# GELU into the output tile, whole-tile instructions and a pinned ACT order in a split GELU-multiply kernel

## Chip, cores and metric

The kernel runs on one core of one Trainium2 chip. The metric is device time in microseconds (us) of one execution. The profile is of one such execution; its span is some 2 us shorter than that execution's time (470.1 against 471.85 before).

## The reference

```python
x = np.random.randn(32, 512, 2048)           # float32
x1, x2 = x[..., :1024], x[..., 1024:]
out = 0.5 * x1 * (1 + erf(x1 / np.sqrt(2))) * x2    # GELU(x1) * x2, float32
```

There are 134.2 MB to read and 67.1 MB to write, and one GELU and one multiply for each output element.

## The kernel before

The rows are cut into 16 tiles of 128 partitions x 8 rows. A partition's 8 rows are adjacent in memory. There are two input tiles and two output tiles. Loads are issued from SP (SyncE), stores from ACT (ScalarE; the last two tiles' from SP), GELU runs on ACT and the multiply on DVE (VectorE).

```python
R = 8
xpool = ctx.enter_context(tc.tile_pool(name="xpool", bufs=2))
opool = ctx.enter_context(tc.tile_pool(name="opool", bufs=2))
# ... load(i): sync.dma_start of a whole tile; store(queue, i, o_tile, rows)
ahead = [load(0), load(1)]
for i in range(n_tiles):
    x_tile = ahead.pop(0)
    o_tile = opool.tile([P, R, half], out.dtype, name="o_tile")
    last = i == n_tiles - 1
    for lo, hi in ((0, 1), (1, 2), (2, 4), (4, 8)) if last else ((0, 4), (4, 8)):
        rows = slice(lo, hi)
        nc.scalar.activation(out=x_tile[:, rows, :half], in_=x_tile[:, rows, :half], func=GELU)
        nc.vector.tensor_mul(out=o_tile[:, rows, :], in0=x_tile[:, rows, :half], in1=x_tile[:, rows, half:])
        if last and hi % 4 == 0:
            store(nc.sync, i, o_tile, slice(hi - 4, hi))
    if not last:
        store(nc.sync if i == n_tiles - 2 else nc.scalar, i, o_tile, slice(0, R))
    if i + 2 < n_tiles:
        ahead.append(load(i + 2))
```

Two rules of reuse follow from this. The load of tile i+2 can be issued only when the multiply of tile i has read its input tile. An output tile can be overwritten only when the store two tiles back has landed.

## Time and profile before

| | before |
|---|---|
| time, median of 3 (lowest to highest) | 471.61 us (471.43 to 471.72) |
| span of the profile | 470.1 us |
| busy: DVE, ACT | 30%, 25% |
| DMA queues' packets, both queues | 99.4% of 16 engines' span |

A queue of transfers must be read with two numbers: how long a transfer takes from issue to landing, and how much of that it spends behind others. The first is in the page's last part; here are the two rows for the bulk of the transfers (the last number is the median in us from issue to landing):

```profile
out_dram<-o_tile ACTq DMA_DIRECT2D x14, 4096.0 KB, 41.6
...
x_tile<-in_x_dram SPq DMA_DIRECT2D x16, 45.4
```

A load takes 45.4 us and a store 41.6, while a load and a store together land every 29 us. So on average 1.6 loads and 1.4 stores are under way: in the steady stretch there is always one of each, and part of the time a second stands behind it.

### The profile page before, as it was taken

What the parts mean: (1) busy time and instruction counts of PE and PEld (TensorE: products, weight loads), DVE (VectorE), ACT (ScalarE), POOL (GpSimd) and SP (SyncE); (2) the same over time, 40 slices, a digit from 0 to 9 for tenths busy, and PEclk for the clock granted to TensorE, in tenths of its full rate; (3) what the DMA queues carried; (4) which work ended last, traced back from release to release, by engine and by line L of the source; (5) the groups of instructions that cost most, each with busy time, mean ns of one, the idle gap of its engine ahead of it and who ended that gap; (6) DMA issues with size and microseconds to landing.
All of it is one profiled execution on the core that took longest, in us unless ns stands there. A gap on an engine that the chain in (4) does not pass through costs nothing.

```text
span 470.1 us, 217 instructions
## 1 busy us (share of the span) xinstructions
DVE 140.5 (30%) x34; ACT 115.4 (25%) x35; POOL 0.2 (0%) x4
## 2 busy tenths in 40 slices
DVE  0070703307043070420705106061150601507042
ACT  1051406024060230603206032060410605105060
POOL 0000000000000000000000000000000000000000
DMA  8999999999999999999999999999999999999988
GB/s 357 446 446 357 443 449 446 402 443 449 402 446 441 435 457 404 432 418 485 407 424 421 488 407 413 432 488 407 402 443 482 413 402 443 472 424 402 480 380 346
DMA packets 4754, 201.35 MB, mean 428 GB/s; under 512 B 528, under 2 KB 528, under 8 KB 528
## 3 DMA queue, kind: packets, MB, share of 16 engines
q1 hardware_dynamic: 2736, 142.61, 70.5%
q10 hardware_dynamic: 2016, 58.72, 28.9%
q14 instruction: 2, 0.02, 0.0%
HBM read 134.22 MB, written 67.11 MB: 428 GB/s over the span
## 4 chain that ended last, share of the span: by engine, by line
DMA 77%; DVE 14%; ACT 7%; issue 0%; ACTq 0%; SPq 0%
DMA x_tile<-in_x_dram 77%; DVE o_tile L58 14%; ACT x_tile L55 7%; ACTq L94 0%; SPq L42 0%; ACTq L55 0%
## 5 line engine op out<-in xcount | busy, mean ns | idle before, releaser
L58 DVE TENSOR_TENSOR o_tile<-x_tile 128x4096 f32<-128x4096 f32 (+2 forms) x34 | 140.5, 4171 | 321.2 <-ACT x_tile L55 321.2
L55 ACT ACTIVATE x_tile<-x_tile 128x4096 f32<-128x4096 f32 (+2 forms) x34 | 114.2, 3407 | 341.0 <-DMA x_tile<-in_x_dram 341.0
L55 ACT ACT_TABLE_LOAD x1 | 1.3, 1283 | 0.7 <-PEq L83 0.7
L83 POOL MEMSET const-bfloat16-1.0<- 128x1 bf16 x1 | 0.1, 102 | 0.0
L83 POOL MEMSET const-uint8-127<- 128x1 uint8 x1 | 0.1, 102 | 0.0
L83 POOL MEMSET const-float32-0.0<- 128x1 f32 x1 | 0.1, 99 | 0.2 <-issue 0.2
L83 POOL MEMSET const-float32-1.0<- 128x1 f32 x1 | 0.1, 99 | 0.0
## 6 DMA issues: line engine op xcount, KB each, us to landing
out_dram<-o_tile ACTq DMA_DIRECT2D x14, 4096.0 KB, 41.6
out_dram<-o_tile SPq DMA_DIRECT2D x1, 4096.0 KB, 24.8
out_dram<-o_tile SPq DMA_DIRECT2D x2, 2048.0 KB, 8.0
x_tile<-in_x_dram SPq DMA_DIRECT2D x16, 45.4
```

The source lines that it names most:

```text
L55: nc.scalar.activation(out=x_tile[:, rows, :half], in_=x_tile[:, rows, :half], func=GELU)
L58: nc.vector.tensor_mul(out=o_tile[:, rows, :], in0=x_tile[:, rows, :half], in1=x_tile[:, rows, half:],)
L83: nc = _bacc.Bacc("TRN2", target_bir_lowering=False, num_devices=1)
```

## The change

The change writes GELU to the output tile and multiplies there in place, handles tiles 1 to 14 with one GELU and one multiply each, joins the first two small steps of the last tile, and asks the scheduler to keep GELU at its place in program order, behind the store before it. The intent is fewer instructions and no second write into the input tile.

```diff
-        for lo, hi in ((0, 1), (1, 2), (2, 4), (4, 8)) if last else ((0, 4), (4, 8)):
+        if last:
+            steps = (0, 2), (2, 4), (4, 8)
+        else:
+            steps = ((0, 4), (4, 8)) if i == 0 else ((0, 8),)
+        for lo, hi in steps:
             rows = slice(lo, hi)
-            nc.scalar.activation(
-                out=x_tile[:, rows, :half], in_=x_tile[:, rows, :half], func=GELU
+            tc.keep_in_program_order(
+                nc.scalar.activation(
+                    out=o_tile[:, rows, :], in_=x_tile[:, rows, :half], func=GELU
+                )
             )
             nc.vector.tensor_mul(
                 out=o_tile[:, rows, :],
-                in0=x_tile[:, rows, :half],
+                in0=o_tile[:, rows, :],
                 in1=x_tile[:, rows, half:],
             )
```

## The prediction

> **What bounds the kernel now.** I read the page first: it says which resource has no free time.
>
> ```profile
> span 470.1 us, 217 instructions
> DVE 140.5 (30%) x34; ACT 115.4 (25%) x35; POOL 0.2 (0%) x4
> ...
> DMA  8999999999999999999999999999999999999988
> ...
> q1 hardware_dynamic: 2736, 142.61, 70.5%
> q10 hardware_dynamic: 2016, 58.72, 28.9%
> ...
> HBM read 134.22 MB, written 67.11 MB: 428 GB/s over the span
> ```
>
> The two compute engines are busy 30% and 25% of the span; the DMA row is 9 (90% or more) in all but three slices. The two queues' packets take 70.5% + 28.9% = 99.4% of the time of the 16 DMA engines: 0.6% of 470.1 us, some 3 us, is all the idle time there is. q1 holds the loads (and the last tiles' stores), q10 the other stores. The bytes are what the reference needs (134.2 MB in, 67.1 MB out, each once).
>
> The chain of waits must be read beside that. It lists compute in every second tile:
>
> ```profile
> 161.26 3.62 ACT x_tile L55
> 164.88 0.02 issue
> 164.91 8.77 DVE o_tile L58 x2
> 173.68 0.02 issue
> 173.70 45.52 DMA x_tile<-in_x_dram
> 219.22 0.02 issue
> 219.24 0.02 ACTq L55
> 219.25 0.04 issue
> 219.30 3.62 ACT x_tile L55
> ```
>
> A load takes 45.52 us from issue to landing, but 8.39 MB (134.22 MB over 16 loads) at 433 GB/s would need 19.4 us. So the link is mostly queueing. The chain is a closed loop with stretchable DMA pieces, not a row of fixed costs. The test is the rate over whole periods. A tile comes every 29.04 us (tile i+2's GELU starts 58.04 us after tile i's: 161.26, 219.30). Cut into such periods, the table by stretches says:
>
> ```profile
> 58.00:87.04 29.04, 8.76 (x2) 7.12 (x2) 0.00 (x0) 1.00 1.00 433
> ...
> 203.20:232.24 29.04, 8.76 (x2) 7.12 (x2) 0.00 (x0) 1.00 1.01 436
> ...
> 377.44:406.48 29.04, 8.76 (x2) 7.12 (x2) 0.00 (x0) 1.00 1.00 432
> ```
>
> The last two columns are DMA share and GB/s: share 1.00, 432 to 436 GB/s, while DVE works 8.76 and ACT 7.12 of 29.04 us. The kernel is bound by the rate of the DMA engines from the first load to the last store.
>
> **What the Trainium skill says.** "DMA: Bandwidth & Descriptors", section "Where 436 GB/s comes from", puts the ceiling of a core's 16 ports at 435.2 GB/s; the periods above are at it. The same page, "Queues, rings and completion order", says each DMA engine round-robins between its queues by packet. The trace agrees: load and store progress together, one 8.39 MB load and one 4.19 MB store landing per period, and neither queue starves. "VectorE: DVE Perf Modes", section on the TRN2 errata, gives (N+151)/0.96 ns for an fp32 two-tensor operation: 4424 ns at N = 4096, where the trace has 4422. "ScalarE: Activation LUTs", section "What ACT_TABLE_LOAD costs", gives 186 + 0.833 N ns without pointer operands: 3598 ns at 4096, where the trace has a mean of 3608.
>
> **The change part by part.** The durations come from the groups by shape:
>
> ```profile
> L58 DVE TENSOR_TENSOR o_tile<-x_tile 128x4096 f32<-128x4096 f32 x31 | 135.8, 4422 | 304.6 <-ACT x_tile L55 304.6
> L55 ACT ACTIVATE x_tile<-x_tile 128x4096 f32<-128x4096 f32 x31 | 110.4, 3608 | 320.6 <-DMA x_tile<-in_x_dram 320.6
> ...
> L58 DVE TENSOR_TENSOR o_tile<-x_tile 128x2048 f32<-128x2048 f32 x1 | 2.3, 2293 | 0.4 <-ACT x_tile L55 0.4
> ...
> L55 ACT ACTIVATE x_tile<-x_tile 128x2048 f32<-128x2048 f32 x1 | 1.9, 1895 | 0.0
> ```
>
> *Whole-tile instructions, tiles 1 to 14.* Two instructions of 4096 elements become one of 8192 on each engine. Extrapolated from these rows: ACT 3608 + 4096 x (3608 - 1895)/2048 = 7034 ns (the page's formula: 7010); DVE 4422 + 4096 x (4422 - 2293)/2048 = 8680 ns (8691). Busy time hardly changes: ACT 7.12 to 7.02, DVE 8.76 to 8.69. What changes is overlap: the multiply now waits for the whole GELU. From landing to freed tile it was 12.50 us (219.24 to 231.74, where the load and store are issued); it becomes 0.06 + 7.02 + 0.02 + 8.69 + 0.02 = 15.81, so **3.3 us longer per tile**, in 14 tiles.
>
> Does that reach the DMA? A load issued at 231.74 stands behind its predecessor, which lands at 248.3 (the next GELU starts at 248.35): 16.6 us of slack. The store issued at 231.74 stands behind the store issued at 202.80, which lands 41.7 us later, at 244.5: 12.8 us of slack. Both exceed 3.3; they shrink to about 13.3 and 9.5 us, and the DMA engines see no gap. The loads' time to landing should fall from 45.4 to about 42.1 us, the stores' from 41.6 to about 38.3, with landings at the same moments. Cost: 0.
>
> *GELU to the output tile.* ACT now waits until the store two tiles back has left that buffer; before, DVE waited for it, later. The load and store issued together at 231.74 take 45.6 and 41.7 us: the store lands at 273.4, the load at 277.3. As the GELU needs the load anyway, the new wait ends 3.9 us before the one that binds. Cost: 0. Reading o_tile rather than x_tile in the multiply changes no rate I can point to. Loads still wait only for the multiply.
>
> *The pin.* Instruction order on ACT is GELU, store, GELU, store in both kernels; DVE and the loading queue keep their order too. Against before it changes nothing.
>
> *First tile.* Still halves; first store and third load go out at 35.2 us as before.
>
> *Last tile.* Steps of 1, 1, 2, 4 rows become 2, 2, 4. The last load lands at 449.8, and then DMA alone sets the end: the store of tile 14 (issued 434.78, 24.8 us to landing) lands at 459.6, and the two half stores of 2.10 MB at 433 GB/s take 4.84 us each, so 464.4 and 469.3. The second was issued at 461.7 and took 7.6 us (the least in the stores' view): 469.3, which agrees. After the change, the GELUs start at 449.9 and take 1.9 + 1.9 + 3.6 us, less some 0.2 of overlap, to 457.1; the last multiply ends at 457.1 + 4.4 = 461.5 (before 461.66), where its store must be queued before 464.4. The multiply of rows 2 to 4 ends at 449.9 + 1.9 + 2 x 2.3 = 456.4 (before 456.0), needed by 459.6. The store of tile 14 is issued 3.3 us later, at about 438.1, but queues behind the last load until 449.8. Cost: 0.
>
> Sum: 0 on the path. The prediction is the time before, **471.6 us**.
>
> **The rivals.** *The longer compute stage lands on the path.* Taken literally, the chain crosses compute 8 times; seven whole-tile crossings x 3.3 = 23 us, 495 us, 5% slower. For it: the chain lists these stages. Against it: the DMA rows have no idle time, and the slack is 16.6 and 12.8 us. *The store wait moved to ACT binds.* If stores drifted 4 us later against loads, ACT would stall. Even then a whole load and a store would be queued while it waits, so the stall would be absorbed; a few tenths of a us, 472 to 473. *Fewer instructions save time.* 14 on each engine, about 0.1 us each: 1.4 us of ACT and 1.0 of DVE, on engines idle 70% of the time: 471.6. *DMA becomes more efficient* because engine and transfer traffic coincide differently. The rate is at 433 to 436 against a ceiling of 435.2; the 201.3 MB at 435.2 GB/s alone need 462.6 us, and 2% faster is 462.2. So it cannot be 2% faster; a gain would be under 2 us.
>
> **Range and chances.** The three runs before span 0.3 us. I allow 0.7 us down for start and tail, and 0.9 up because the slacks shrink: 470.9 to 472.5. Faster by 2% is excluded by bytes over rate: 0.005. Slower by 2% (9.4 us) would need the DMA engines idle for 0.67 us in each of 14 tiles, though 9.5 us of slack is left: 0.02. Within 2%: 0.975.
>
> **What would show it right or wrong.** Right: ACT instructions of 7.0 us and DVE of 8.7 us; DMA row at 9 throughout; periods still 29.04 us at 433 GB/s; loads' time to landing about 42 us and stores' about 38; ACT's waits put down to the load, not to a store; last store landing near 469.3. Wrong: a period above 29.04 us with GB/s below 430, ACT waiting for a store, or a gap in the DMA after 459 us. I would then have mistaken queued work for slack, or the order in which the two queues drain would have changed.

## The result, and the profile after

| | before | after |
|---|---|---|
| time, median (lowest to highest), 6 runs each | 471.67 (471.43 to 472.30) | 471.71 (471.35 to 473.43) |
| ratio | | 1.0005 (95%: 0.9989 to 1.0022) |
| span of the profile | 470.1 | 469.6 |

Ratios here and below are the mean time of one kernel's runs over that of the other's of the same rounds, so they are not quite the ratio of the medians. Executions over 1.5% slower than the fastest of the same kernel are left out of the means.

The page of the changed kernel, lines that the prediction showed of the kernel before:

```profile
DVE 139.4 (30%) x19; ACT 114.0 (24%) x20; POOL 0.2 (0%) x4
...
DMA  8999999999999999999999999999999999999998
...
q1 hardware_dynamic: 2736, 142.61, 70.5%
q10 hardware_dynamic: 2016, 58.72, 29.0%
```

Fifteen instructions fewer on each engine (14 from whole tiles, one from the last tile), and the DMA row is as full as it was. The groups by shape, with the new 8192-element rows:

```profile
L65 DVE TENSOR_TENSOR o_tile<-o_tile,x_tile 128x8192 f32<-128x8192 f32 x14 | 121.7, 8692 | 280.7 <-ACT o_tile L61 280.7
L61 ACT ACTIVATE o_tile<-x_tile 128x8192 f32<-128x8192 f32 x14 | 98.4, 7029 | 300.5 <-DMA x_tile<-in_x_dram 300.5
```

One tile in the chain of waits (start us, duration us, what), to be held against the same stretch of the kernel before:

```profile
160.86 7.04 ACT o_tile L61
...
167.93 8.70 DVE o_tile L65
...
176.65 42.16 DMA x_tile<-in_x_dram
```

GELU starts at 160.86 where it started at 161.26, and the next load is issued at 176.65 where it was issued at 173.70. The load then takes 42.16 us in place of 45.52. The issue is late by 2.95 us and the landing early by 0.41 (218.81 against 219.22, the end of the link in each chain): the link gave back all that the compute stage took. The times to landing say it for all transfers:

```profile
out_dram<-o_tile ACTq DMA_DIRECT2D x14, 4096.0 KB, 38.3
...
x_tile<-in_x_dram SPq DMA_DIRECT2D x16, 42.1
```

And a stretch of one period, with DMA share and GB/s in the last two columns, is as it was:

```profile
377.44:406.48 29.04, 8.71 (x2) 7.03 (x1) 0.00 (x0) 1.00 1.00 434
```

### The profile page after: what moved, and what is told of

It is laid out like the page before. It is cut to its first block, busy times and chain, and to the rows that moved or that the text cites. A ratio compares the mean times of both kernels' runs of the same rounds, so it can differ in the third digit from the quotient of the medians.

```text
span 469.6 us, 177 instructions
## 1 busy us (share of the span) xinstructions
DVE 139.4 (30%) x19; ACT 114.0 (24%) x20; POOL 0.2 (0%) x4
## 4 chain that ended last, share of the span: by engine, by line
DMA 72%; DVE 14%; ACT 12%; ACTq 0%; issue 0%; SPq 0%
DMA x_tile<-in_x_dram 72%; DVE o_tile L65 14%; ACT o_tile L61 12%; ACTq L101 0%; SPq L43 0%; ACTq L61 0%
## 5 line engine op out<-in xcount | busy, mean ns | idle before, releaser
L65 DVE TENSOR_TENSOR o_tile<-o_tile,x_tile 128x8192 f32<-128x8192 f32 (+2 forms) x19 | 139.4, 7344 | 321.8 <-ACT o_tile L61 321.8
L61 ACT ACTIVATE o_tile<-x_tile 128x8192 f32<-128x8192 f32 (+2 forms) x19 | 112.7, 5949 | 342.0 <-DMA x_tile<-in_x_dram 342.0
## 6 DMA issues: line engine op xcount, KB each, us to landing
out_dram<-o_tile ACTq DMA_DIRECT2D x14, 4096.0 KB, 38.3
x_tile<-in_x_dram SPq DMA_DIRECT2D x16, 42.1
```

The costliest lines, as they stand in the source:

```text
L61: nc.scalar.activation(out=o_tile[:, rows, :], in_=x_tile[:, rows, :half], func=GELU)
L65: nc.vector.tensor_mul(out=o_tile[:, rows, :], in0=o_tile[:, rows, :], in1=x_tile[:, rows, half:],)
```

## The experiments

The theory: the DMA engines always have a load and a store to work on, so a longer compute stage only shortens the time that transfers stand in line (**slack**). The main rivals: parts of the change that cancel, compute on the path as the chain of waits suggests, and the wait for stores that ACT took over. Each kernel's result was correct.

| run | time, median us | ratio to before (95%) |
|---|---|---|
| no pin | 475.69 | 1.0090 (1.0073 to 1.0107) |
| whole tiles alone (with the pin) | 471.64 | 1.0003 (0.9988 to 1.0018) |
| output-tile GELU alone | 471.73 | 1.0006 (0.9991 to 1.0021) |
| one more DVE pass | 471.78 | 1.0005 (0.9988 to 1.0021) |
| two more DVE passes | 551.96 | 1.1705 (1.1671 to 1.1739) |
| one input buffer: before, after | 718.67, 767.94 | 1.5240, 1.6285 |
| one output buffer: before, output-tile GELU alone, after | 651.13, 704.69, 752.18 | 1.3808, 1.4944, 1.5951 |
| whole tiles, no pin | 477.78 | 1.0138 (1.0121 to 1.0155) |
| first tile split | 483.31 | 1.0247 (1.0232 to 1.0262) |

### The parts one by one

Whole-tile instructions alone (the changed kernel, GELU back in the input tile; the pin and the last tile's steps stay):

```diff
-                    out=o_tile[:, rows, :], in_=x_tile[:, rows, :half], func=GELU
+                    out=x_tile[:, rows, :half], in_=x_tile[:, rows, :half], func=GELU
-                in0=o_tile[:, rows, :],
+                in0=x_tile[:, rows, :half],
```

> Whole-tile instructions alone: GELU still written in place into the input tile. Theory 1: 471.7 us, ratio to before within 0.3%; time from landing to freed tile 15.8 us, loads' time to landing 42.1, stores' 38.3 as in the changed kernel. Rival (two effects that cancel: whole tiles cost some us, the output-tile GELU or the pin gains as much): this run is slower than before by more than 0.5% and the next one faster.

GELU to the output tile alone (the same edit the other way round, in the kernel before):

> GELU to the output tile alone, half-tile instructions as before. Theory 1: 471.7 us, within 0.3%; landing to freed tile 12.5 us and loads' time to landing 45.4 as before; ACT waits for loads only, because the store two tiles back has landed 3.9 us before the load. Rival (cancelling effects): faster than before by more than 0.5%, or ACT waiting for stores.

Measured: 471.64 and 471.73 us, neither apart from before by more than its interval. With whole tiles alone loads took 42.1 us to landing and stores 38.4; with output-tile GELU alone 45.5 and 41.8. In both, ACT waited for loads only. The rival of two effects that cancel is out: the output-tile GELU is worth nothing by itself, and so are whole tiles with the pin (without it see below). The pin alone, on the kernel before, was not run.

### A longer compute stage, with the rest left alone

```diff
+            for _ in range(1 if 0 < i and not last else 0):     # 2 in the second run
+                nc.vector.tensor_tensor(out=o_tile[:, rows, :], in0=o_tile[:, rows, :],
+                                        in1=o_tile[:, rows, :], op=mybir.AluOpType.max)
             nc.vector.tensor_mul(
```

> The changed kernel with one needless DVE pass (o = max(o, o), 8.69 us) ahead of the multiply in tiles 1 to 14; the result stays right. Time from landing to freed tile 15.8 + 8.7 = 24.5 us. Theory 1 (slack: loads have 13.2 us left, stores 9.4): 471.7 us, at most 473; loads' time to landing falls by 8.7 to about 33.4 us, stores' to about 29.6; DVE busy rises by 122 to about 261 us. Rival (the compute stages in the chain of waits are on the path): the chain crosses 7 such tiles, 7 x 8.7 = 61 us more, 533 us.

Measured: 471.78 us. (A fourth run took 494.59 us, was slow and is left out.) DVE worked 261.1 us in place of 139.4 and the time did not move. The waits of this run (engine, line, waited for: us in total, times, longest):

```profile
ACT o_tile L61 <- DMA out_dram<-o_tile: 285.7, 13, 22.1
```

Here the wait that the change moved to ACT is the one that ends last, in 13 of 16 tiles, and it costs nothing. The trace's landings show by how little: store and load land 0.2 us apart (217.43 and 217.26 us). Loads took 33.3 us to landing, as expected; stores 33.5, not the 29.6 expected. In the trace the store of tile 1 was issued at 69.13 us and the store before it landed at 69.79. By these times the store queue, with hardly any slack left, ran short for a moment; the loads went ahead (tile 2's landed at 72.25, not 73.86), and the stores' lead of 3.9 us was gone from then on. What kept the time was that the DMA engines still had a load and a store to work on while ACT waited: in the steady stretch the next ones were issued at 212.99 and 212.96, more than 4 us before the landings at 217.26 and 217.43. A link through compute in the chain is by itself no evidence of cost: this run's chain has DVE at 27% of the span, twice that of the changed kernel.

> Two needless DVE passes in tiles 1 to 14: landing to freed tile 15.8 + 17.4 = 33.2 us, more than the 29.04 us that the DMA engines need for a tile's bytes; DVE itself is busy 26.1 us a tile, less than 29.04. Theory 1 with its limit: ACT takes GELU, store, GELU, store in order, so a tile's GELU cannot start before the multiply of the tile before it is done; the compute stage becomes the period at about 33.6 us. 44.9 + 14 x 33.6 + 7.2 + 4.4 + 7.7 + 2.2 = about 537 us, with gaps in the DMA row. Rival (DMA-bound whatever the latency, as long as no engine is busy for more than 29.04 us): 472 us.

Measured: 551.96 us, 17% slower, so the slack has an end where the theory put it. The timeline (start us, us, engine, line, operation, idle time before it and its releaser) and the DMA row:

```profile
145.66 7.03 ACT L61 ACTIVATE o_tile<-x_tile 128x8192 f32<-128x8192 f32 x1 [26.68 <-DVE o_tile L72]
...
170.17 8.69 DVE L72 TENSOR_TENSOR o_tile<-o_tile,x_tile 128x8192 f32<-128x8192 f32 x1
178.89 0.37 ACTq L47 DMA_DIRECT2D out_dram<-o_tile  x1
179.36 7.03 ACT L61 ACTIVATE o_tile<-x_tile 128x8192 f32<-128x8192 f32 x1 [26.68 <-DVE o_tile L72]
```

```profile
DMA  9999949889797998969969889898988969889358
```

GELU of one tile starts right after the store of the tile before: 33.7 us from one to the next (expected 33.6), each compute stage in series, and the DMA row has holes. The slack is gone too: the load at 145.22 us goes out 1.3 us after the one before it landed (143.97). The estimate of 537 us was 15 us too low because of the end: the built order puts the last tile's first multiply ahead of tile 14's, so tile 14's passes are done at 507.2 us but DVE's next instruction starts at 516.9, and tile 14's store goes out at 527.8. So the stage can grow from 12.5 us to 24.5 at no cost, and at 33.2, run in series by ACT's order, it sets the period. The point at which it turns was not measured, nor what would happen without that order.

### The change without its slack

```diff
-xpool = ctx.enter_context(tc.tile_pool(name="xpool", bufs=2))
+xpool = ctx.enter_context(tc.tile_pool(name="xpool", bufs=1))
-    ahead = [load(0), load(1)]
+    ahead = [load(0)]
-        if i + 2 < n_tiles:
-            ahead.append(load(i + 2))
+        if i + 1 < n_tiles:
+            ahead.append(load(i + 1))
```

> The kernel before with one input buffer in place of two: no load can be queued behind another, so the slack is gone. Theory 1: load and store go out together and share the engines, about 31 us, then 12.5 us from landing to freed tile with idle DMA engines: period about 43.5 us, about 695 us in all.

> The changed kernel with one input buffer. Theory 1: here the 3.3 us per tile of whole-tile instructions are on the path: period about 46.8 us, about 741 us, that is 46 us (7%) slower than the kernel before with one input buffer. Rival (the change costs nothing by itself, the slack has no part in it): both kernels with one input buffer take the same time.

Measured: 718.67 us for the kernel before and 767.94 for the changed one. The levels are some 25 us above the estimates, mostly because a load beside a store took 32.3 us (median), not 31; the difference, 49.3 us, or 3.3 us for each of 15 later tiles, is the one expected (46). With the second input buffer the same 3.3 us cost nothing. (The two kernels differ in the whole change, not in whole tiles alone.) The loss of overlap is real, and the second buffer hides it.

The same with one output buffer (`opool` with `bufs=1`, nothing else):

> The kernel before with one output buffer in place of two: the multiply waits for the store of the tile before to land, GELU does not. Estimate: load and store go out together, land after about 31 us, then 8.8 us of multiplies: period about 39.8 us, about 640 us. For comparison with the changed kernel with one output buffer, where GELU waits for the store too: period 31 + 15.8 = 46.8 us, about 740 us. If the new wait of ACT costs nothing even when it binds, the two would differ by the whole-tile cost alone, 3.3 us a tile.

> One output buffer, half-tile instructions, GELU to the output tile: only that part of the change. From a store's landing to the next store's issue: half a GELU 3.6 + 8.8 = 12.4 us against 8.8. Theory 1: 15 x 3.6 = 55 us more than the kernel before with one output buffer, about 706 us, so that some 50 of the 105 us belong to the output-tile GELU and some 50 to the whole tile. Rival: near 651 us.

> The changed kernel with one output buffer. In the kernel before with one output buffer (651 us) only the multiplies, 8.8 us, stood between a store's landing and the next store's issue; here GELU waits for the landing too, so 7.0 + 8.7 + 0.1 = 15.8 us stand there. Theory 1 (the change trades away overlap that only the second buffer makes worthless): 15 x 7.0 = 105 us more, about 755 us. Rival (the moved wait costs nothing in itself, only the whole-tile instructions lose overlap): in the kernel before with one output buffer GELU was done before the multiply began, so the whole tile would cost nothing there either and the time would be near 651 us.

Measured: 651.13, 704.69 and 752.18 us. The output-tile GELU costs 53.6 us here (55 expected), and whole tiles, with the pin and the last tile's steps, a further 47.5 (some 50 expected). The waits say how. First the kernel before with one output buffer, then the changed one:

```profile
DVE o_tile L58 <- DMA out_dram<-o_tile: 475.7, 15, 34.9
```

```profile
ACT o_tile L61 <- DMA out_dram<-o_tile: 605.2, 15, 43.5
```

In the first, DVE waits for the store while GELU is already done in the input tile. In the second, GELU itself waits, and its time adds to the store's. So the prediction's reading of the moved wait was right in both halves: it is stricter than the old one, and with two output buffers it doesn't bind.

### The pin

```diff
-            tc.keep_in_program_order(
-                nc.scalar.activation(out=o_tile[:, rows, :], in_=x_tile[:, rows, :half], func=GELU)
-            )
+            nc.scalar.activation(out=o_tile[:, rows, :], in_=x_tile[:, rows, :half], func=GELU)
```

> The changed kernel without the pin. The built order shows what it does: on ACT the GELU of tiles 5, 9, 12 (roughly every third or fourth tile) now stands ahead of the store of the tile before, so at these places two stores go out together, one of them about 20 us late (13.3 us until the next load lands plus 7.0 us of GELU). Theory 1 (slack absorbs: the DMA engines always have a whole load queued): still 471 to 474 us, period 29.0 us on average, but stores' time to landing and ACT's waits irregular, and ACT waiting for stores now and then. Rival (the pin is what keeps the change flat; a late store stalls the GELU two tiles on, through the output buffer, and that holds the next load back): each such place costs up to 9 us, so 480 to 510 us.

(The built order is the order in which the scheduler left the instructions on each engine.) Measured: 475.69 us, 0.9% slower than before. Neither side had it quite: the time is above theory 1's range by 1.7 us and far below the rival's. The timeline at tiles 5 and 6 (the second line merges two stores, the later one issued at 174.99; in the trace late stores stand at tiles 5, 9 and 13):

```profile
159.21 7.03 ACT L60 ACTIVATE o_tile<-x_tile 128x8192 f32<-128x8192 f32 x1 [20.58 <-DMA x_tile<-in_x_dram]
159.23 16.12 ACTq L47 DMA_DIRECT2D out_dram<-o_tile  x2
...
190.66 7.03 ACT L60 ACTIVATE o_tile<-x_tile 128x8192 f32<-128x8192 f32 x1 [24.42 <-DMA out_dram<-o_tile]
```

The store of tile 4 was ready at 147.4 us, when its multiply ended, but stands behind GELU of tile 5 in ACT's order and goes out at 159.2: 11.9 us late. (The 20 us expected were too many: the queue issues the store as soon as GELU has started, not when it is done.) GELU of tile 6 then waits for that store. Is that wait the cost? The last experiment of this group takes it away, with GELU back in the input tile and still no pin:

> Whole-tile instructions, GELU in place in the input tile, no pin. The built order has the same late stores on ACT as the changed kernel without the pin (475.7 us against 471.5), so the late stores come with whole-tile instructions, whatever GELU writes. If the 4 us there come from the late stores themselves (engines without stores to move for a while, and the tail): 474 to 476 us here too. If they come from GELU waiting for late stores through the output buffer: GELU waits for no store here, only the multiply does, 7 us later, so 471.5 to 473 us.

Measured: 477.78 us, 1.4% slower, with ACT waiting for loads only; the same kernel with the pin (whole tiles alone) took 471.64. So the late stores cost the time without any wait of GELU for the output buffer. The late stores come with whole-tile instructions (the built order is the same for both), and the kernel before, with half-tile instructions and no pin, has none.

Where the 4 to 6 us go can be told in part, from the profiled runs, which were the fastest of each kernel (474.14 and 475.43 us). In the run without the pin no DMA engine is idle in the steady stretch, yet the packets took 1.9 us more in all on each DMA engine than in the changed kernel, out of 2.3 us by which the span is longer. In the second run the packets took 0.5 us more, and the other 3.0 of its 3.5 us are idle time of DMA engines after 455 us. There the last output-tile store on ACT's queue landed at 454.2 us, after the last load, where it lands at 447.0 with the pin; the first multiply of the last tile waited for it, 0.6 us beyond the end of its GELU.

One more reading of the traces goes with this. A transfer is done when the last of its 16 semaphore updates has come, which by their number is one from each DMA engine. In the changed kernel the 16 updates of a load lie within 0.8 to 1.2 us of each other from the first tile to the last. In these two runs the spread grows after the first late store: in the first from 0.7 to as much as 3.6 us, in the second from 2.4 to 5.4 us at the last load. Read so, the engines fall out of step. Whether that makes the packets slower or comes of it is open.

### A try at a version that beats both

In the changed kernel each of the 16 DMA engines moves 8 load packets and 8 store packets per tile, and where the two alternate the trace has 2.418 us for a load packet of 64 KB and 1.213 us for a store packet of 32 KB: 16 x 8 x (2.418 + 1.213) = 464.8 us for the whole kernel. If packets get no faster than that, no reordering gains more than some 5 us of the 469.6. Part of it is in the first 40 us, where loads run alone and their packets take 2.54 us on average. So, on the reading that this is how loads alone run, the first tile was loaded and stored in halves, to start storing sooner:

```diff
-        nc.sync.dma_start(out=x_tile, in_=x_t[i])
+        for lo, hi in ((0, 4), (4, 8)) if i == 0 else ((0, R),):
+            nc.sync.dma_start(out=x_tile[:, lo:hi, :], in_=x_t[i][:, lo:hi, :])
...
-            if last and hi % 4 == 0:
-                store(nc.sync, i, o_tile, slice(hi - 4, hi))
-        if not last:
+            if (last or i == 0) and hi % 4 == 0:
+                store(nc.sync if last else nc.scalar, i, o_tile, slice(hi - 4, hi))
+        if not last and i > 0:
```

> An attempt to beat both: the changed kernel with the first tile loaded in two halves and stored in two halves, so that the first store goes out near 21 us instead of 35 us. The load packets of the first 40 us, when no store runs, took 2.50 to 2.59 us instead of 2.42 (16 packets on each DMA engine, so about 1.9 us lost in all); where load and store packets alternate they take 2.42. Theory 1 (rate of the DMA engines sets the time, the slow start is a property of loads alone): up to 1 us less, 470.5 to 471.5 us, ratio 0.998 to 1.000. Rival (the first packets are slow whatever runs beside them; splitting only adds DMAs): 471.5 to 472 us.

Measured: 483.31 us (five runs, 482.54 to 484.30), 2.5% slower, which neither side expected. A stretch of 29 us of this run:

```profile
364.00:393.00 29.00, 8.69 (x1) 7.03 (x1) 0.00 (x0) 1.00 1.00 421
```

The DMA share is 1.00 as before, but the rate is 421 GB/s in place of 434, long after the first tile; from 45 to 451 us it is 425, against 433 in the changed kernel. The engines are not idle; the packets are slower: load packets of 64 KB average 2.495 us, against 2.434 in the changed kernel, and one in fourteen takes over 2.9 (one in 68 there). The packets make up 8.3 of the 11.1 us by which the span is longer.

The reading on which this try rested was wrong, as the trace of the changed kernel shows. Its average of the first 40 us hides two bursts: the first load packet on each DMA engine took 2.9 to 3.5 us for 15 of 16, and 16 packets that started at 38.5 to 39.4 us, the last before the first store's packets, took 3.2 to 4.0. The 208 packets between 4 and 35 us, also with loads alone, took 2.42 us like those beside stores. So there was no slowness of loads alone to be cured.

Here ACT waits for stores in 14 of 16 tiles and stores land 0.2 to 2.1 us after the loads they run beside, which is also so in the run with one more pass (0.2 us) at full rate, so that alone is not the cause. What differs is how the two queues' packets lie against each other, and how far the DMA engines are out of step: the 16 updates of a load spread over 1.7 us at tile 1 and 6.8 us at the last tile. Which of these sets the rate, or whether they only come with it, was not found. This kernel doesn't beat either.

## Why the prediction was right

It gave 471.6 us, range 470.9 to 472.5; measured were 471.71 against 471.67 before. That the two medians lie within about 0.1 us of the forecast is closer than the noise allows one to claim: the changed kernel's six runs span 2.1 us, and one of them (473.43) lies above the range. By its steps:

- **The bound.** The DMA share was 1.00 and the rate 434 GB/s in the period shown of the changed kernel. (By the prediction's own sum the period is 58.04/2 = 29.02 us, not 29.04; nothing hangs on it.) That the chain's compute links are not costs here is shown by the run with one more pass: 8.7 us more in 14 tiles, no change in time.
- **Durations.** 7034 and 8680 ns were extrapolated; 7029 and 8692 measured. ("VectorE: DVE Perf Modes" states its formula for an add, at N of 512 and 2048; that it also fits this multiply at 8192, 8691 ns, is what this trace adds.) From 160.78, when the load landed in the trace, to the next issue at 176.65 are 15.87 us, against 15.81 predicted.
- **The slack.** Predicted 13.3 us for loads and 9.5 for stores after the change. In the changed kernel the load issued at 176.65 stands behind one that lands at 190.0 (13.4), the store behind one that lands at 186.0 (9.4). Times to landing of 42.1 and 38.3 us are those predicted, to the tenth.
- **The moved wait.** ACT waited for loads only. Its margin in the trace is 3.8 us (store landed at 215.03, load at 218.81), against 3.9 predicted. That a bound wait would be absorbed was an argument then; the run with one more pass shows it, for engines that still had a load and a store to work on.
- **The tail.** The last store was predicted to be issued at 461.5 and to land at 469.3; in the trace it was issued at 461.2 and landed at 468.9, with the landings of the two half stores 4.86 us apart (predicted 4.84), as expected of an end that DMA alone sets.
- **The pin.** "Against before it changes nothing" held, but said too little. Whole-tile instructions without it cost 0.9 to 1.4%. The pin pays for a reordering that the whole tiles bring.
- **A rival misjudged.** The prediction looked at a changed efficiency of the DMA engines only as a gain, "under 2 us". Two runs, the one without the pin and the one with a split first tile, show that a loss of that kind is possible, in the second the larger part of 2.5%. That the changed kernel kept the rate of the kernel before was assumed by the prediction, not worked out: in this the outcome owes something to luck.

## What to carry to other kernels

Before pricing a longer compute stage, take the time between a transfer's issue and its predecessor's landing, in every queue that must stay full. Delays within that slack (3.3 us, and 12.0 us in all with one more pass) cost nothing, and with the slack taken away 3.3 us a tile counted in full. Larger instructions gave up overlap for fewer instructions, which bought nothing with the engines busy 25% and 30% of the span; writing an intermediate into the output tile trades a free buffer for a stricter wait. When instruction sizes change, compare the built order on each engine too: a store that slips behind the next tile's work cost more here than all parts of the change together. And look at single packets before an average of them: two bursts looked like a slow start.

## What the Trainium skill lacked or had wrong

- "DMA: Bandwidth & Descriptors" gives one ceiling for busy engines and a round-robin between queues, but nothing on how the pattern of two queues sets the rate. At a DMA share of 1.00 the changed kernel moved 433 GB/s from 45 to 451 us and the one with a split first tile 425; load packets of 64 KB averaged 2.434 us in the one and 2.495 in the other.
- "SBUF — State Buffer", in its summary of rules, has ~358 GB/s for transfers between HBM and SBUF. One core working alone moved 429 GB/s over the whole span here, as "HBM Reference" says it can (≈425).
- No page has the test that decided this, slack in a queue: 45.4 us from issue to landing shrank to 42.1 and 33.3 us at one and the same kernel time.
